# The passage from FFN1 into the mixer in one written order, and the first chunk's product in the gate's buffer

## The chip, the cores and the metric

One core of a Trainium2 chip runs the whole program in one launch. The metric is the time of the program on the device in microseconds (us); lower is better.

## The reference

One layer of a decoder on 512 tokens of width 1024, all in float32:

```
x = x + 1/2 * rms_norm(swiglu(rms_norm(x, ffn1_pre)), ffn1_post)
x = x +       rms_norm(mixer (rms_norm(x, mix_pre)),  mix_post)
x = x + 1/2 * rms_norm(swiglu(rms_norm(x, ffn2_pre)), ffn2_post)

rms_norm(x, g) = x * rsqrt(mean(x*x) + 1e-6) * g
swiglu(h)      = (silu(gate) * up) @ w_down      # gate, up = halves of h @ w_gu; 2 * 2816 columns
mixer(h):  z = h @ w_in                          # 512 pooling, 512 query, 2 * 128 key and value columns
           windowed pooling | 128-wide windowed attention, each rms-normed, then @ w_out
```

## The kernel before

Every matmul operand is split into a high part (a copy by ACT, L166) and a low part (raw minus high, by DVE or POOL, L169); a product is three matmuls, high by high, low by high and high by low (`mm3`, L359 to L361). The 512 tokens lie in 4 blocks `x0` to `x3` of 128.

An FFN has two stages. `gate_up` computes gate and up in 11 chunks of 256 columns. Chunk 0 is done plainly in eight blocks (names `f_c`; f1 and f2 stand for the two FFNs, and the profile writes f for both). Chunks 1 to 10 use a Strassen-like scheme of 7 products in the order 1, 5, 2, 6, 3, 7, 4, in pairs of banks px, py and pz (names f_x, f_y, f_z). They need sums of quarters of the normed input: `token_sums` forms them (`f1f`) and splits them into high and low parts `f1t5`, `f1t6`, `f1t7`, `f1t4` (low parts on DVE, L477). Behind chunk 0 ACT writes silu(gate) into two buffers `s00` and `s01` (tag `sg2`, which has two buffers), and DVE multiplies them by up (L541) into `hs`. The pairs of banks come free only when DVE has read chunk 0's banks, and ACT's first copy of a px (L587) goes into a buffer of tag `sg2` that the product has read.

`down_proj` computes 7 products of half the width in the order 1, 5, 6, 3, 7, 2, 4, from weight tiles `d`. The last product, 4, goes into the banks `xs_`; of its six weight tiles two are used for both halves of the tokens, then four (`tail`) for block 2 and again for block 3. Each block is then post-normed by `post_norm`: squares of both halves on ACT (`j_f1po`), the mean on DVE (`ms_f1po`, L339), the root on POOL (`r_f1po`, L334), gains (L413) and the sum into x (L416) on DVE. For f1 the mixer's pre-norm of the block follows (`j_b`, `r_b`, `xn_b`), and after that the normed block is transposed by PE (`tr_mx`) and split by ACT and DVE into `xT_hi` and `xT_lo` (L397, L400). The mixer's block 0 of queries (`pq0`, 24 matmuls of 512 columns) and of keys and values (`pkv0`, 24 of 256 columns) follows, with weights `wq0` to `wq3`, `wkv0`, `wkv1`; then block 1 (`pq1`, `pkv1`).

PE runs in the order in which the code is written. `in_order()` does the same for DVE, ACT and POOL; outside of it a scheduler orders those three when the program is built. Before the change the last product of `down_proj` and the passage into the mixer stand outside. Weights are loaded by SP's DMA queue in a fixed order (`W`), into eight buffers; `W.more(n)` issues loads and casts for n more, and `W.run_ahead` says how many loads go ahead of the casts. POOL's own DMA queue sums weights in `gate_up`. `power` is the root on POOL, and `pcols` is a transpose of 12 rows of factors into columns that the mixer's later parts read.

Of the kernel before, what the change touches and what calls it, by code (L numbers as in the profile page):

```python
# [10 lines left out]
F32 = mybir.dt.float32  # L11
# [8 lines left out]
P = 128  # L20
# [47 lines left out]
def trunk_layer(  # L68
# [262 lines left out]
    def power(ms, name):  # L331

        r = sm.tile([P, 1], F32, tag="r", name=f"r_{name}")
        nc.gpsimd.tensor_tensor(r, ms, half, ALU.pow)  # L334
        return r

    def mean_square(ss2, eps, name):
        ms = sm.tile([P, 1], F32, tag="ms", name=f"ms_{name}")
        nc.vector.scalar_tensor_tensor(ms, ss2[:, 0:1], eps, ss2[:, 1:2], ALU.add, ALU.add)  # L339
        return ms  # L340
# [39 lines left out]
                between()  # L380
        return xn

    def pre_norm(t, g, name, xn=None):
        r = power(mean_square(sizes(t, name), EPS, f"{name}{t}"), f"{name}{t}")
        return scaled(t, r, g, name, xn=xn)

    def transposes(t, xn, xT, name):
        for h in range(2):
            ps = bank(f"tr_{name}{t}{h}")
# [14 lines left out]
    def halves(g):  # L404
        return g[:, :512], g[:, 512:]

    def post_norm(t, parts, tmp, g, scale, name, dst=None):

        ss2 = squares(parts, ROOT / scale, f"{name}{t}")
        r = power(mean_square(ss2, EPS / (scale * scale), f"{name}{t}"), f"{name}{t}")  # L410
        for n in range(2):
            at = slice(n * 512, (n + 1) * 512)
            nc.vector.tensor_tensor(tmp[n], parts[n], g[:, at], ALU.mult)  # L413
        for n in range(2):
            at = slice(n * 512, (n + 1) * 512)
            nc.vector.scalar_tensor_tensor(xs[t][:, at], tmp[n], r, xs[t][:, at], ALU.mult, ALU.add)  # L416
            if dst is not None:
                nc.sync.dma_start(dst[:, at], xs[t][:, at])
# [39 lines left out]
    def token_sums(xq, name):  # L458

        parts, full = xq  # L460
        out = {1: parts[0, 0], 2: parts[1, 0], 3: parts[1, 1]}
        for p in (5, 6, 7, 4):
            out[p] = act_pair(f"{name}t{p}", (P, 4, 256))
        sums = {}
        for q in range(2):
            b11, b12, b21, b22 = (full[i][q] for i in ((0, 0), (0, 1), (1, 0), (1, 1)))
            nc.vector.tensor_tensor(b11, b11, b12, ALU.subtract)
            nc.vector.tensor_tensor(b12, b22, b12, ALU.subtract)
            nc.vector.scalar_tensor_tensor(b22, b22, -1.0, b11, ALU.mult, ALU.subtract)
            nc.vector.scalar_tensor_tensor(b21, b21, -1.0, b22, ALU.mult, ALU.subtract)  # L470
            sums[q] = {5: b11, 7: b12, 6: b22, 4: b21}
        for p in (5, 6, 7, 4):
            hi, lo = out[p]
            for q in range(2):
                at = (slice(None), slice(2 * q, 2 * q + 2))
                nc.scalar.copy(hi[at], sums[q][p])
                nc.vector.tensor_tensor(lo[at], sums[q][p], hi[at].bitcast(F32), ALU.subtract)  # L477
        return out

    def product_late(ps, w, xt, first, last):  # L480

# [23 lines left out]
    def gate_up(name, xq, hs, between):  # L505
# [18 lines left out]
                block(i)  # L524
        for i in range(4, 8):
            block(i)
        xs_ = token_sums(xq, name)
        W.hi, W.lo = nc.scalar, nc.vector
        W.run_ahead = 3
        W.more(2)  # L530
# [7 lines left out]
        for j in range(2):  # L538
            sg = wk.tile([P, 2, 256], F32, tag="sg2", bufs=2, name=f"{name}_s0{j}")
            nc.scalar.activation(sg, banks[0, j].rearrange("p (h t) -> p h t", h=2), AF.Silu, scale=-1.0)  # L540
            nc.vector.scalar_tensor_tensor(  # L541
                hs[0][:, 2 * j : 2 * j + 2, 0], banks[1, j].rearrange("p (h t) -> p h t", h=2), -1.0,
                sg, ALU.mult, ALU.mult,
            )
        use_banks(f"{name}_pairs", 4)

        def h_of(c):
# [65 lines left out]
        use_banks(f"{name}_banks", 8)  # L613
        return begin, [on_act[-1], on_dve[-1]]

    def down_proj(name, hs, ends, g_post, between, done):

# [49 lines left out]
                elif i == 2:  # L669
                    nc.vector.tensor_tensor(kept[1][:, t], zs_[t], kept[1][:, t], ALU.add)  # L670

        def normed(t):
            first = kept[1][:, t] if t < 2 else xs_[t - 2]
            second = kept[6][t] if t < 2 else kept[5][:, t - 2]
            dst = out[0, t * P : (t + 1) * P, :] if name == "f2" else None
            tmp = slots_of["pool"].tile([P, 512], F32, tag="k", bufs=2, name=f"{name}_n{t}") if t >= 2 else first
            post_norm(t, [first, second], [tmp, second], g_post, 0.5, f"{name}po", dst)
            done(t)

        NW = (NCH + 1) // 2  # L680
        with behind(ends[0]):
# [2 lines left out]
        with behind(ends[1]):  # L684
            form(1, 2)
            W.get(f"{name}_d10")
        with in_order():
            for at, i in enumerate(PRODUCTS[:-1]):
                for n in range(NW):
                    w = W.get(f"{name}_d{i}{n}")  # L690
                    if n % 2 == 0:
                        form(PRODUCTS[at + 1], n // 2)
                    multiply(i, n, w)
                    if n == 0 and at:
                        put_away(PRODUCTS[at - 1])
        i = PRODUCTS[-1]
        for n in range(2):
            multiply(i, n, W.get(f"{name}_d{i}{n}"))
            if n == 0:
                put_away(PRODUCTS[-2])  # L700
        normed(0)
        normed(1)
        tail = [W.get(f"{name}_d{i}{n}", 0) for n in range(2, NW)]
        if name == "f1":
            W.run_ahead = 3
            W.more(2)
        for t in range(2):
            for n, w in enumerate(tail):
                multiply(i, n + 2, w, (t,))
                if t and n == 1:  # L710
                    between(1)
            if t and name == "f1":
                W.more(2)
            normed(t + 2)
            if t == 0:
                between(0)
        use_slots(f"{name}_end", HB)


    xq = quarters("f1")  # L720
# [118 lines left out]
    xT2 = []  # L839
    xns = {}  # L840

    def done1(t):
        xn = ap.tile([P, 2, 512], F32, tag=("ahi", "alo")[t % 2], name=f"xn_b{t}")
        xns[t] = pre_norm(t, g3, "b", [xn[:, n] for n in range(2)])

    def between1(t):
        if t == 0:
            xT2.extend(act_pair(f"xT2_{i}") for i in range(4))
        transposes(t, xns[t], xT2, "mx")

    pcols = bank("pcols")
    nc.tensor.transpose(pcols[:, :12], rows, ident[:12, :12])
    nc.vector.tensor_copy(cols, pcols[:, :12])
    nc.vector.tensor_tensor(cols[:, 4:8], cols[:, 0:4], cols[:, 4:8], ALU.mult)
    down_proj("f1", hs, ends, g2, between1, done1)

    def project(ps, t, nm, per):
        for k in range(KD):
# [222 lines left out]
        next(pi[g])  # L1081

    def mixer():
        nc.scalar.copy(wph, wpr)
        nc.gpsimd.tensor_tensor(wpl, wpr, wph.bitcast(F32), ALU.subtract)
        qkv_block(0, lambda: None)
        qkv_out(0)
        transposes(2, xns[2], xT2, "mx")
        qkv_block(1, lambda: transposes(3, xns[3], xT2, "mx"))
        qkv_out(1)  # L1090
        turn(0)
        W.run_ahead = 2
        W.lo = nc.gpsimd
        qkv_block(2, lambda: (scores(0), tops(0), turn(1), exps(0, 0), exps(0, 1)))
        qkv_out(2)
        normalise(0)
        qkv_block(3, lambda: (W.more(2), scores(1), tops(1), turn(2), exps(1, 0)))
        W.more(2)
        turn_probs(0, 0)
        turn_probs(0, 1)  # L1100
        exps(1, 1)
        qkv_out(3)
        run(3)
        normalise(1)
        scores(2)
        run(3)
        tops(2)
        pool_sums(3)
        values(0, 0)
        values(0, 1)  # L1110
        turn(3)
        exps(2, 0)

        turn_probs(1, 0)
        attn_out(0)
        run(2)
        scores(3)
        exps(2, 1)
        tops(3, (0,))
        values(1, 0)  # L1120
        turn_probs(1, 1)
        normalise(2)
        tops(3, (1,))
        run(2)
        values(1, 1)
        pool_sums(2)
        W.lo = nc.vector

        turn_probs(2, 0)
        attn_out(1)  # L1130
        exps(3, 0)
        pool_mid(3)
        run(1)
        W.more(1)
        attn_rms(0)
        values(2, 0)
        turn_probs(2, 1)
        exps(3, 1)
        normalise(3)
        run(1)  # L1140
        pool_sums(1)
        yT[0:2] = [act_pair(f"yT{i}") for i in (0, 1)]
        pool_out(3, True)
        values(2, 1)

        turn_probs(3, 0)
        attn_rms(1)
        attn_out(2)
        W.more(1)
        pool_mid(2)  # L1150
        run(0)
        values(3, 0)
        turn_probs(3, 1)
        run(0)
        pool_sums(0)
        W.more(2)
        pool_out(2)
        values(3, 1)
        pool_mid(1)
        pool_mid(0)  # L1160
        attn_rms(2)
        attn_out(3)
# [118 lines left out]
    hs2 = []  # L1281
    ends = gate_up("f2", xq2, hs2, last_steps)
    g6 = gain(ffn2_post, "g6")
    down_proj("f2", hs2, ends, g6, lambda t: None, lambda t: None)


# [27 lines left out]
```

## Time and profile before

| | us |
|---|---|
| median of 3 runs (lowest, highest) | 867.23 (865.86, 867.49) |
| the profiled execution | 867.36 |
| its span in the trace | 865.6 |
| PE busy in it | 826.5 (95%) |
| DVE, ACT, POOL busy | 662.3, 468.3, 204.4 |
| mean granted clock of TensorE | 0.988 |

The engines are PE (matmuls), DVE (vector), ACT (scalar), POOL (GpSimd) and SP (which issues DMAs). A row of the timeline has the start, the duration, the engine, the line, the operation, its output and inputs, and in brackets how long the engine had been idle and what released it. A row of a group has the number of operations, the busy time, the mean in ns, and the idle time before them. A row of PE's waits has the total, the number and the longest. A row of a window has the stretch, the summed busy time and that of PE, PE's weight loads, DVE, ACT and POOL, then the granted clock, the DMA share and GB/s.

### The profile page before, as it was taken

The page shows a single profiled execution, that of the slowest core. Times are in us where ns is not written, and L with a number is a line of the kernel's source. Part 1 is how long each engine was busy: PE and PEld are TensorE (multiplying, and loading weights), DVE is VectorE, ACT ScalarE, POOL GpSimd, SP SyncE. Part 2 cuts the span into 40 slices and gives each one's busy share as a digit, 9 for nine tenths or more (in the row PEclk, how much of TensorE's full clock was granted, in tenths as well). Part 3 has the DMA queues.
Part 4 walks back from the last instruction along what each step waited for, and adds up shares of the span by engine and source line. Part 5 has one row for each costly group of instructions (what it writes and reads, how often), then busy time and mean ns, then how long its engine had stood idle before and what let it go on. Part 6 is the DMA issues. An engine that isn't in the chain of part 4 may idle for free. (4 is left out here: it accounts for less than half of the span.)

```text
span 865.6 us, 14043 instructions
## 1 busy us (share of the span) xinstructions
PE 826.5 (95%) x5525; PEld 755.2 (87%) x5525; DVE 662.3 (77%) x856; ACT 468.3 (54%) x743; POOL 204.4 (24%) x287
## 2 busy tenths in 40 slices
PE   7989999999999999789999998799999999999996
PEld 5889999999988878578878878799999999988785
DVE  6968887778987798744666779578888888877895
ACT  5644444454555575545996567344544445555662
POOL 4103334433310000123532011033333333300001
PEclk9999999999999999999999999999999999999999
DMA  9428888888885558312005402258899887955552
GB/s 305 122 69 217 230 233 221 225 235 237 233 262 182 183 190 260 110 28 71 26 25 147 145 25 74 66 159 237 222 240 232 235 241 221 252 198 173 175 163 97
DMA packets 96877, 150.77 MB, mean 174 GB/s; under 512 B 6948, under 2 KB 53676, under 8 KB 96812
## 3 DMA queue, kind: packets, MB, share of 16 engines
q1 hardware_dynamic: 77100, 103.74, 38.0%
q0 software_dynamic: 19712, 46.15, 22.5%
q8 instruction: 43, 0.70, 0.3%
q14 instruction: 22, 0.18, 0.1%
HBM read 147.77 MB, written 48.23 MB: 226 GB/s over the span
## 5 line engine op out<-in xcount | busy, mean ns | idle before, releaser
L571 POOL DMA_DIRECT2D f_t<-in_ffn_w_down x132 | 89.6, 751 | 80.7 <-issue 47.8
L169 DVE TENSOR_TENSOR f_d_lo<-f_d_raw,f_d_hi 128x1024 fp32r<-128x1024 f32 x84 | 92.1, 1130 | 8.8 <-ACT f_d_hi L166 8.1
L166 ACT CAST f_d_hi<-f_d_raw 128x1024 fp32r<-128x1024 f32 x84 | 79.0, 978 | 15.6 <-PE f_z L361 14.7
L568 POOL COPY f_k<-f_h 1x1 f32<-1x1 f32 x18 | 21.0, 1165 | 192.8 <-DVE f_h L560 192.8
L595 ACT COPY f_h<-f_y 128x512 f32<-128x512 f32 x20 | 11.7, 587 | 80.8 <-PE f_y L361 80.8
L603 ACT ACTIVATE f_s<-f_s 128x1024 f32<-128x1024 f32 x20 | 21.2, 1061 | 41.5 <-DVE f_s L602 41.5
L571 POOL DMA_DIRECT2D f_t<-f_t x44 | 32.1, 798 | 37.0 <-issue 30.6
L600 ACT COPY f_s<-f_x 128x512 f32<-128x512 f32 x20 | 11.7, 587 | 48.4 <-PE f_x L361 48.4
L635 ACT CAST f2e_hi<-f_h 128x1024 fp32r<-128x1024 f32 (+1 forms) x21 | 20.4, 977 | 30.9 <-DVE f_h L632 7.7
L635 ACT CAST f1e_hi<-f_h 128x1024 fp32r<-128x1024 f32 (+1 forms) x21 | 20.4, 976 | 30.9 <-DVE f_h L632 7.7
L359 PE MATMUL f_x<-f_d_hi,f1e_hi 128*128 128x512 f32 x88 | 35.1, 398 | 1.2 <-DVE f_h L611 1.2
L360 PE MATMUL f_x<-f_d_lo,f2e_hi 128*128 128x512 f32 x88 | 34.4, 391 | 0.8 <-DVE f_d_lo L169 0.8
L360 PE MATMUL f_x<-f_d_lo,f1e_hi 128*128 128x512 f32 x88 | 34.6, 393 | 0.5 <-DVE f_d_lo L169 0.5
L359 PE MATMUL f_x<-f_d_hi,f2e_hi 128*128 128x512 f32 x88 | 34.4, 390 | 0.7 <-DVE f_h L611 0.7
L587 ACT COPY f_s<-f_x 128x512 f32<-128x512 f32 x20 | 11.7, 586 | 42.5 <-PE f_x L361 39.8
L361 PE MATMUL f_x<-f_d_hi,f1e_lo 128*128 128x512 f32 x88 | 34.5, 392 | 0.0
L361 PE MATMUL f_x<-f_d_hi,f2e_lo 128*128 128x512 f32 x88 | 34.3, 389 | 0.0
L636 DVE TENSOR_TENSOR f1e_lo<-f_h,f1e_hi 128x1024 fp32r<-128x1024 f32 (+1 forms) x21 | 23.7, 1132 | 11.4 <-ACT f1e_hi L635 11.4
L636 DVE TENSOR_TENSOR f2e_lo<-f_h,f2e_hi 128x1024 fp32r<-128x1024 f32 (+1 forms) x21 | 23.6, 1133 | 11.4 <-ACT f2e_hi L635 11.4
L334 POOL TENSOR_TENSOR r_f1po<-ms_f1po,half 128x1 f32<-128x1 f32 x4 | 3.5, 865 | 107.8 <-DVE ms_f1po L339 107.8
L334 POOL TENSOR_TENSOR r_f2po<-ms_f2po,half 128x1 f32<-128x1 f32 x4 | 3.5, 865 | 106.6 <-DVE ms_f2po L339 106.6
L359 PE MATMUL po<-wo_hi,yT_hi 128*128 128x512 f32 x64 | 25.3, 395 | 0.0
(1026 smaller groups left out, 3421.8 us busy)
## 6 DMA issues: line engine op xcount, KB each, us to landing
f_t<-in_ffn_w_down POOLq DMA_DIRECT2D x132, 256.0 KB, 6.2
f_d_raw<-f_t SPq DMA_DIRECT2D x40, 512.0 KB, 4.6
f_d_raw<-in_ffn_w_down SPq DMA_DIRECT2D x30, 512.0 KB, 4.2
f_t<-f_t POOLq DMA_DIRECT2D x44, 256.0 KB, 6.6
f_raw<-in_ffn_w_gu SPq DMA_DIRECT2D x8, 512.0 KB, 7.6
x<-in_x SPq DMA_DIRECT2D x4, 512.0 KB, 8.2
f_d_raw<-f_t SPq DMA_DIRECT2D x8, 256.0 KB, 3.7
wq_raw<-in_w_in SPq DMA_DIRECT2D x4, 512.0 KB, 4.2
```

The lines of the kernel that those rows point to most:

```text
L166: nc.scalar.copy(hi, src)
L169: self.lo.tensor_tensor(lo, src, hi.bitcast(F32), ALU.subtract)
L359: nc.tensor.matmul(ps, wh, xh, start=first, stop=False, skip_group_check=open_)
L360: nc.tensor.matmul(ps, wh, xlo, start=False, stop=False, skip_group_check=open_)
L361: nc.tensor.matmul(ps, wlo, xh, start=False, stop=last, skip_group_check=open_)
L568: then = nc.gpsimd.tensor_copy(tick, hs[(c - 1) // 4][:1, 0, (c - 1) % 4, :1]).ins
L571: nc.gpsimd.dma_start(to, part, accum_op=op, max_dma_last_dim=2048)
L587: on_act.append(nc.scalar.copy(sg[:, :, a], px[:, :, a]).ins)
L595: on_act.append(nc.scalar.copy(h[1], py[:, :, a]).ins)
L603: on_act.append(nc.scalar.activation(sg, sg, AF.Silu, scale=-1.0).ins)
L635: nc.scalar.copy(hi, src)
L636: nc.vector.tensor_tensor(lo, src, hi.bitcast(F32), ALU.subtract)
```

## The change

- `gate_up`: the product up * silu(gate) of chunk 0 is written in place into the gate's buffer (L534 of the new program), and POOL copies it from there into `hs[0]` (L537). `token_sums` becomes a generator; it is left after the sums and product 5's split, and the splits for products 6, 7 and 4 come behind the second product.
- `down_proj`: `post_norm` and `pre_norm` are taken apart into sizes, gains, roots and sums. The squares of all blocks' second halves, and the gains of blocks 0 and 1's, are done during product 2; blocks 0 and 1 have their roots side by side. The squares of a whole FFN's post-norm share one tile.
- The passage: everything from the last product to `pq0`, `pkv0` and the norm of block 3 is in one `in_order()`, written by hand with `steps` that f1 hands in. The transposes of block 0 move from ahead of block 3's matmuls to behind the second of its four tiles, block 1's from there to behind its last tile, and block 2's from ahead of `pq1` to between `pq0` and `pkv0`. The weight casts come one at a time; `wq3_lo` and `wkv0_lo` are made by POOL instead of DVE. Block 3's sum, sizes and norm are in the mixer.
- The factor columns (`pcols`, a copy and a product on DVE) move from ahead of f1's `down_proj` into the mixer, ahead of `pq1`. On SP's queue the load of the pooling weights (`wpr`) moves from behind the `wu` loads to between `wkv0`'s and `wkv1`'s.
- FFN2 uses the same `down_proj` with no `steps`.

What the queues then hold, first DVE behind FFN2's first chunk. Before (`f2f101` is a sum of `token_sums`, `f2t` are splits, `f2_1b_raw` a sum of chunk 1's weights, `f2_h0` is `hs[0]`):

```order
L470 SCALAR_TENSOR_TENSOR f2f101_5365<-f2f101_5365,f2f111_5367 128x512
L477 TENSOR_TENSOR f2t6_lo_5754<-f2f110_5366,f2t6_hi_5753 128x512
L477 TENSOR_TENSOR f2t7_lo_5756<-f2f010_5362,f2t7_hi_5755 128x512
L219 TENSOR_TENSOR f2_1b_raw_5787<-f2_1a_raw_5501,f2_1b_raw_5787 128x1024
L477 TENSOR_TENSOR f2t7_lo_5756<-f2f011_5363,f2t7_hi_5755 128x512
L477 TENSOR_TENSOR f2t6_lo_5754<-f2f111_5367,f2t6_hi_5753 128x512
L477 TENSOR_TENSOR f2t4_lo_5758<-f2f100_5364,f2t4_hi_5757 128x512
L477 TENSOR_TENSOR f2t4_lo_5758<-f2f101_5365,f2t4_hi_5757 128x512
L541 SCALAR_TENSOR_TENSOR f2_h0_5808<-f2_c10_5586,f2_s00_5811 128x2x256
L541 SCALAR_TENSOR_TENSOR f2_h0_5808<-f2_c11_5611,f2_s01_5814 128x2x256
```

And after:

```order
L461 SCALAR_TENSOR_TENSOR f2f101_5367<-f2f101_5367,f2f111_5369 128x512
L534 SCALAR_TENSOR_TENSOR f2_s00_5801<-f2_c10_5588,f2_s00_5801 128x512
L219 TENSOR_TENSOR f2_1b_raw_5777<-f2_1a_raw_5503,f2_1b_raw_5777 128x1024
L534 SCALAR_TENSOR_TENSOR f2_s01_5805<-f2_c11_5613,f2_s01_5805 128x512
L470 TENSOR_TENSOR f2t6_lo_5756<-f2f110_5368,f2t6_hi_5755 128x512
L470 TENSOR_TENSOR f2t6_lo_5756<-f2f111_5369,f2t6_hi_5755 128x512
L470 TENSOR_TENSOR f2t7_lo_5758<-f2f010_5364,f2t7_hi_5757 128x512
```

The two products now stand ahead of all six low parts; the weight sum stands between them.

ACT in the passage, before (`wq` and `wkv` are the casts of weights, `j_b2` the squares of block 2's pre-norm, two for a block, `j_f1po` those of the post-norm, `xT2` the transposed blocks):

```order
L166 CAST wq2_hi_3894<-wq2_raw_3766 128x1024
L353 ACTIVATE j_b11_3752,ss2_b1_3749<-x1_89 128x512
L166 CAST wq3_hi_3900<-wq3_raw_3768 128x1024
L353 ACTIVATE j_f1po20_3803,ss2_f1po2_3802<-f1_x0_2945 128x512
L353 ACTIVATE j_f1po21_3805,ss2_f1po2_3802<-f1_p5_3221 128x512
L353 ACTIVATE j_b20_3817,ss2_b2_3816<-x2_90 128x512
L353 ACTIVATE j_b21_3819,ss2_b2_3816<-x2_90 128x512
L353 ACTIVATE j_f1po30_3906,ss2_f1po3_3905<-f1_x1_2946 128x512
L397 CAST xT2_0_hi_3827<-tr_mx00_3835 128x2x128
```

And after:

```order
L166 CAST wq2_hi_3851<-wq2_raw_3756 128x1024
L353 ACTIVATE j_b20_3858,ss2_b2_3857<-x2_90 128x512
L353 ACTIVATE j_b21_3860,ss2_b2_3857<-x2_90 128x512
L677 ACTIVATE j_f1po30_3871,f1_sso_2945<-f1_x1_2944 128x512
L393 CAST xT2_0_hi_3823<-tr_mx10_3879 128x2x128
L393 CAST xT2_1_hi_3825<-tr_mx10_3879 128x2x128
L393 CAST xT2_2_hi_3827<-tr_mx11_3888 128x2x128
L393 CAST xT2_3_hi_3829<-tr_mx11_3888 128x2x128
L166 CAST wq3_hi_3899<-wq3_raw_3758 128x1024
L166 CAST wkv0_hi_3945<-wkv0_raw_3771 128x1024
L166 CAST wkv1_hi_3960<-wkv1_raw_3849 128x1024
```

The cast `wq3_hi` stood ahead of the squares of block 2 and stands now behind them, block 3's first squares and the four high parts of block 1's transposes; `wkv0_hi` and `wkv1_hi` follow it directly.

POOL in the passage, before:

```order
L334 TENSOR_TENSOR r_f1po0_3717<-ms_f1po0_3715,half_106 128x1
L334 TENSOR_TENSOR r_b0_3731<-ms_b0_3729,half_106 128x1
L334 TENSOR_TENSOR r_f1po1_3742<-ms_f1po1_3740,half_106 128x1
L334 TENSOR_TENSOR r_b1_3756<-ms_b1_3754,half_106 128x1
L334 TENSOR_TENSOR r_f1po2_3809<-ms_f1po2_3807,half_106 128x1
L334 TENSOR_TENSOR r_b2_3823<-ms_b2_3821,half_106 128x1
L334 TENSOR_TENSOR r_f1po3_3912<-ms_f1po3_3910,half_106 128x1
L1085 TENSOR_TENSOR wpl_3941<-wpr_3938,wph_3940 128x512
L334 TENSOR_TENSOR r_b3_3926<-ms_b3_3924,half_106 128x1
```

And after:

```order
L334 TENSOR_TENSOR r_f1po0_3707<-ms_f1po0_3705,half_106 128x1
L334 TENSOR_TENSOR r_f1po1_3712<-ms_f1po1_3710,half_106 128x1
L334 TENSOR_TENSOR r_b0_3754<-ms_b0_3752,half_106 128x1
L334 TENSOR_TENSOR r_b1_3769<-ms_b1_3767,half_106 128x1
L334 TENSOR_TENSOR r_f1po2_3809<-ms_f1po2_3807,half_106 128x1
L334 TENSOR_TENSOR r_f1po3_3877<-ms_f1po3_3875,half_106 128x1
L169 TENSOR_TENSOR wq3_lo_3900<-wq3_raw_3758,wq3_hi_3899 128x1024
L169 TENSOR_TENSOR wkv0_lo_3946<-wkv0_raw_3771,wkv0_hi_3945 128x1024
L334 TENSOR_TENSOR r_b2_3951<-ms_b2_3949,half_106 128x1
L334 TENSOR_TENSOR r_b3_4040<-ms_b3_4038,half_106 128x1
L1155 TENSOR_TENSOR wpl_3915<-wpr_3912,wph_3914 128x512
```

Roots of blocks 0 and 1 now stand in pairs, and the two subtractions of 128x1024 stand ahead of block 2's root, for whose norm `xn_b2` the transposes between `pq0` and `pkv0` wait.

The diff, cut to its core:

```diff
         for p in (5, 6, 7, 4):
+            if p == 6:
+                yield out
...
-        xs_ = token_sums(xq, name)
+        to_sum = token_sums(xq, name)
+        xs_ = next(to_sum)
...
-            nc.vector.scalar_tensor_tensor(
-                hs[0][:, 2 * j : 2 * j + 2, 0], banks[1, j].rearrange("p (h t) -> p h t", h=2), -1.0,
-                sg, ALU.mult, ALU.mult,
+            done = nc.vector.scalar_tensor_tensor(
+                sg, banks[1, j].rearrange("p (h t) -> p h t", h=2), -1.0, sg, ALU.mult, ALU.mult
             )
+            nc.gpsimd.tensor_copy(hs[0][:, 2 * j : 2 * j + 2, 0], sg)
+        with behind([done.ins]):
+            next(to_sum, None)
...
+        sizes_ = sm.tile([P, 2 * NT], F32, tag="ls", bufs=2, name=f"{name}_sso")
+        tmp, rs = {}, {}
+        def half_of(t, n):
+            if t < 2:
+                return (kept[1][:, t], kept[6][t])[n]
+            return (xs_[t - 2], kept[5][:, t - 2])[n]
+        def half_size(t, n):
+            junk = wk.tile([P, 512], BF16, tag="junk", bufs=1, name=f"j_{name}po{t}{n}")
+            nc.scalar.activation(
+                junk, half_of(t, n), AF.Square, scale=2 * ROOT, accum_out=sizes_[:, 2 * t + n : 2 * t + n + 1]
+            )
+        def half_gain(t, n):
+            part = half_of(t, n)
+            tmp[t, n] = part
+            if t >= 2 and n == 0:
+                tmp[t, n] = slots_of["pool"].tile([P, 512], F32, tag="k", bufs=2, name=f"{name}_n{t}")
+            nc.vector.tensor_tensor(tmp[t, n], part, g_post[:, n * 512 : (n + 1) * 512], ALU.mult)
+        def post_root(t):
+            rs[t] = power(mean_square(sizes_[:, 2 * t : 2 * t + 2], 4 * EPS, f"{name}po{t}"), f"{name}po{t}")
+        def add_to_x(t):
             dst = out[0, t * P : (t + 1) * P, :] if name == "f2" else None
+            add_normed(t, (tmp[t, 0], tmp[t, 1]), rs[t], dst)
...
+        mix = steps if name == "f1" else {}
+        def then(step, t):
+            if step in mix:
+                mix[step](t)
...
+                    if i == 2 and 1 <= n <= 4:
+                        half_size(n - 1, 1)
+                        if n <= 2:
+                            half_gain(n - 1, 1)
+            i = PRODUCTS[-1]
+            w = W.get(f"{name}_d{i}0")
+            multiply(i, 0, w)
+            put_away(2)
+            for t in range(2):
+                half_size(t, 0)
+            for t in range(2):
+                half_gain(t, 0)
+                post_root(t)
+            w = W.get(f"{name}_d{i}1")
+            multiply(i, 1, w)
+            for t in range(2):
+                add_to_x(t)
+                then("size", t)
+            tail = [W.get(f"{name}_d{i}{n}", min(3, NW - 1 - n)) for n in range(2, NW)]
+            then("root", 0)
+            then("weights", 0)
+            then("norm", 0)
+            then("root", 1)
+            then("weights", 1)
+            then("norm", 1)
+            for t in (2, 3):
+                half_gain(t, 1)
             for n, w in enumerate(tail):
+                multiply(i, n + 2, w, (0,))
+            half_size(2, 0)
+            half_gain(2, 0)
+            post_root(2)
+            for n, w in enumerate(tail):
+                multiply(i, n + 2, w, (1,))
+                if n == 1:
+                    then("turn", 0)
+                    then("weights", 2)
+                    add_to_x(2)
+                    then("size", 2)
+            half_size(3, 0)
+            half_gain(3, 0)
+            post_root(3)
+            then("turn", 1)
+            then("weights", 3)
+            if not mix:
+                add_to_x(3)
...
+    def weights1(n):
+        W.run_ahead = 3
+        W.lo = nc.gpsimd if n == 3 else nc.vector
+        W.more(1)
...
     def mixer():
+        with in_order():
+            W.more(1)
+            W.lo = nc.vector
+            root1(2)
+            norm1(2)
+            add_to_x(3)
+            W.more(1)
+            size1(3)
+            qkv_block(0, lambda: turn1(2))
+            root1(3)
+            norm1(3)
         nc.scalar.copy(wph, wpr)
         nc.gpsimd.tensor_tensor(wpl, wpr, wph.bitcast(F32), ALU.subtract)
-        qkv_block(0, lambda: None)
         qkv_out(0)
-        transposes(2, xns[2], xT2, "mx")
+        pcols = bank("pcols")
+        nc.tensor.transpose(pcols[:, :12], rows, ident[:12, :12])
+        nc.vector.tensor_copy(cols, pcols[:, :12])
+        nc.vector.tensor_tensor(cols[:, 4:8], cols[:, 0:4], cols[:, 4:8], ALU.mult)
         qkv_block(1, lambda: transposes(3, xns[3], xT2, "mx"))
```

More of the change, by code (lines that the diff above doesn't have):

```diff
@@ L381, in scaled @@
         return xn
-    def pre_norm(t, g, name, xn=None):
-        r = power(mean_square(sizes(t, name), EPS, f"{name}{t}"), f"{name}{t}")
-        return scaled(t, r, g, name, xn=xn)
     def transposes(t, xn, xT, name):
@@ L405, in halves, with add_normed @@
         return g[:, :512], g[:, 512:]
[L407 to L413, printed above, removed]
+    def add_normed(t, tmp, r, dst=None):
         for n in range(2):
@@ L477, in token_sums @@
                 nc.vector.tensor_tensor(lo[at], sums[q][p], hi[at].bitcast(F32), ALU.subtract)
-        return out
     def product_late(ps, w, xt, first, last):
@@ L614, in gate_up, with down_proj @@
         return begin, [on_act[-1], on_dve[-1]]
-    def down_proj(name, hs, ends, g_post, between, done):
+    def down_proj(name, hs, ends, g_post, steps):
         forms = {}
@@ L670, in put_away @@
                     nc.vector.tensor_tensor(kept[1][:, t], zs_[t], kept[1][:, t], ALU.add)
-        def normed(t):
-            first = kept[1][:, t] if t < 2 else xs_[t - 2]
-            second = kept[6][t] if t < 2 else kept[5][:, t - 2]
+        sizes_ = sm.tile([P, 2 * NT], F32, tag="ls", bufs=2, name=f"{name}_sso")
[18 more added lines that the diff above has]
+        def add_to_x(t):
             dst = out[0, t * P : (t + 1) * P, :] if name == "f2" else None
-            tmp = slots_of["pool"].tile([P, 512], F32, tag="k", bufs=2, name=f"{name}_n{t}") if t >= 2 else first
-            post_norm(t, [first, second], [tmp, second], g_post, 0.5, f"{name}po", dst)
-            done(t)
+            add_normed(t, (tmp[t, 0], tmp[t, 1]), rs[t], dst)
         NW = (NCH + 1) // 2
@@ L695, in down_proj @@
                         put_away(PRODUCTS[at - 1])
[L696 to L707, printed above, removed]
-            for n, w in enumerate(tail):
[L709 to L716, printed above, removed]
+                    if i == 2 and 1 <= n <= 4:
+                        half_size(n - 1, 1)
+                        if n <= 2:
+                            half_gain(n - 1, 1)
@@ L717, in down_proj @@
+            half_size(3, 0)
[5 more added lines that the diff above has]
+                add_to_x(3)
         use_slots(f"{name}_end", HB)
+        return add_to_x
     xq = quarters("f1")
@@ L840, in trunk_layer, with size1, root1, norm1 @@
     xns = {}
-    def done1(t):
+    sizes1, roots1 = {}, {}
+    def size1(t):
+        sizes1[t] = sizes(t, "b")
+    def root1(t):
+        roots1[t] = power(mean_square(sizes1[t], EPS, f"b{t}"), f"b{t}")
+    def norm1(t):
         xn = ap.tile([P, 2, 512], F32, tag=("ahi", "alo")[t % 2], name=f"xn_b{t}")
-        xns[t] = pre_norm(t, g3, "b", [xn[:, n] for n in range(2)])
-    def between1(t):
+        xns[t] = scaled(t, roots1[t], g3, "b", xn=[xn[:, n] for n in range(2)])
+    def turn1(t):
         if t == 0:
@@ L849, in between1 @@
         transposes(t, xns[t], xT2, "mx")
[L851 to L855, printed above, removed]
+    def weights1(n):
+        W.run_ahead = 3
+        W.lo = nc.gpsimd if n == 3 else nc.vector
+        W.more(1)
+    add_to_x = down_proj(
+        "f1", hs, ends, g2,
+        {"size": size1, "root": root1, "norm": norm1, "turn": turn1, "weights": weights1},
+    )
     def project(ps, t, nm, per):
@@ L1283, in trunk_layer @@
     g6 = gain(ffn2_post, "g6")
-    down_proj("f2", hs2, ends, g6, lambda t: None, lambda t: None)
+    down_proj("f2", hs2, ends, g6, {})
 _INS = [
```

## The prediction, on record before the changed kernel ran

> **What bounds the kernel now.** I read the page's busy shares first, then PE's waits by length, then windows round each long wait, and last the timeline of the engine that PE waits for.
>
> ```profile
> span 865.6 us, 14043 instructions
> PE 826.5 (95%) x5525; PEld 755.2 (87%) x5525; DVE 662.3 (77%) x856; ACT 468.3 (54%) x743; POOL 204.4 (24%) x287
> PE f_x L359 <- DVE f_h L541: 4.6, 1, 4.6
> PE tr_mx L391 <- DVE xn_b L378: 3.9, 1, 3.9
> PE f_y L359 <- ACT f_s L587: 3.2, 1, 3.2
> ```
>
> PE is busy for 826.5 of 865.6 us, so a change that leaves the matmuls alone can win only PE's idle time and what idling does to its clock. Three waits stand out, and the change is at all three: one behind each FFN's first chunk (f_y, f_x) and one in the passage from FFN1 into the mixer (tr_mx). Windows show what follows each; the columns wanted are PE's busy time, the fifth engine's after it, and PEclk.
>
> ```profile
> 46.64:50.98 4.34, 4.34 (x25) 4.34 (x25) 1.23 (x1) 0.89 (x1) 0.00 (x0) 0.64 0.22 56
> 50.98:53.86 2.88, 2.88 (x27) 2.88 (x25) 1.06 (x1) 2.48 (x3) 0.00 (x0) 1.00 0.28 97
> 547.83:552.27 4.44, 4.44 (x24) 4.44 (x25) 0.00 (x0) 0.00 (x0) 0.00 (x0) 0.62 0.02 4
> 356.92:360.62 3.70, 3.70 (x14) 3.27 (x14) 3.26 (x6) 0.54 (x2) 0.86 (x1) 0.54 0.59 177
> 374.00:377.40 3.40, 3.40 (x19) 3.40 (x18) 1.41 (x2) 0.23 (x1) 0.55 (x1) 0.51 0.00 0
> 339.04:377.99 38.95, 30.35 (x140) 24.89 (x138) 29.18 (x50) 21.36 (x52) 7.29 (x10) 0.91 0.38 115
> ```
>
> The 24 matmuls behind the first stall took 4.34 us at a granted clock of 0.64; the next 24 took 2.88 at 1.00, so the stall cost 1.46 more than itself. Behind the second it is 4.44, 1.56 more. The last row is the passage, from the start of the last product to the first matmul of pq1 (the mixer's second query product): 38.95 us, of which PE idles 8.60. The two rows above it lie inside: 3.70 us at 0.54 and 3.40 at 0.51, together some 3.4 us lost to the clock.
>
> **Part A, FFN1's first chunk.** DVE's timeline, and PE's first row after the stall:
>
> ```profile
> 39.67 0.68 DVE L477 TENSOR_TENSOR f1t_lo<-f1f,f1t_hi 128x512 fp32r<-128x512 f32 x1
> 40.27 1.21 DVE L219 TENSOR_TENSOR f_1b_raw<-f_1a_raw,f_1b_raw 128x1024 f32<-128x1024 f32 x1
> 41.41 0.68 DVE L477 TENSOR_TENSOR f1t_lo<-f1f,f1t_hi 128x512 fp32r<-128x512 f32 x1
> 42.01 0.68 DVE L470 SCALAR_TENSOR_TENSOR f1f<-f1f,f1f 128x512 f32<-128x512 f32 x1
> 42.61 2.48 DVE L477 TENSOR_TENSOR f1t_lo<-f1f,f1t_hi 128x512 fp32r<-128x512 f32 x4
> 45.20 1.29 DVE L541 SCALAR_TENSOR_TENSOR f_h<-f_c,f_s 128x512 f32<-128x512 f32 x2
> 46.64 0.55 PE L359 MATMUL f_y<-f1t_hi,f_1p_hi 128*128 128x256 f32 x1 [3.17 <-ACT f_s L587]
> ```
>
> PE stops at 43.47 and starts at 46.64, 0.15 us after the second product (L541) ends: f_y needs the bank that the product frees, so I read the wait as DVE's, though the row names ACT's copy L587, which itself waits for that product. Six low parts (L477), 0.6 us apart, stood ahead of the products and now stand behind. From 39.67 DVE then does the weight sum (1.14 to the next start) to 40.81, the first product to 41.42, L470 to 42.02, the second product to 42.71. PE needs it at 43.47, so there is no stall and nothing cools: 3.17 + 1.46 = 4.63, taken as 4.6. With the clock's part kept it is 3.2.
>
> The new POOL copies into h are not in this trace. The nearest rows are POOL's:
>
> ```profile
> L169 POOL TENSOR_TENSOR f_c_lo<-f_raw,f_c_hi 128x512 fp32r<-128x512 f32 x7 | 10.4, 1506 | 1.0 <-ACT f_c_hi L166 0.8
> L169 POOL TENSOR_TENSOR wu_lo<-wu_raw,wu_hi 128x1024 fp32r<-128x1024 f32 x4 | 9.5, 2390 | 3.7 <-ACT wu_hi L166 3.7
> L1043 POOL TENSOR_TENSOR win<-u 128x511 f32<-128x511 f32 x4 | 4.2, 1038 | 20.5 <-ACT u L1037 20.5
> ...
> L334 POOL TENSOR_TENSOR r_b<-ms_b,half 128x1 f32<-128x1 f32 x4 | 2.2, 548 | 11.9 <-DVE ms_b L339 11.9
> ```
>
> A copy has one input fewer than L1043's 1.04 us, and at most costs f_c_lo's 1.51; I take 1.0. Only ACT's next px copy waits for it: s00's copy starts at 41.4 and ends by 42.9, before the product for px has ended, so it costs nothing. The six low parts run from 42.71 to 46.3; the first two (product 6) end near 44.0, and that product comes 48 matmuls of 0.12 after 43.47, at 49.2. Five microseconds of cover hide them.
>
> **Part B, FFN2's first chunk.**
>
> ```profile
> 541.05 0.69 DVE L470 SCALAR_TENSOR_TENSOR f2f<-f2f,f2f 128x512 f32<-128x512 f32 x1
> ...
> 542.86 1.22 DVE L219 TENSOR_TENSOR f_1b_raw<-f_1a_raw,f_1b_raw 128x1024 f32<-128x1024 f32 x1
> ...
> 546.40 1.28 DVE L541 SCALAR_TENSOR_TENSOR f_h<-f_c,f_s 128x512 f32<-128x512 f32 x2
> 547.83 0.36 PE L359 MATMUL f_x<-f2b_hi,f_1p_hi 128*128 128x256 f32 x1 [4.60 <-DVE f_h L541]
> ```
>
> Here DVE does L470 until 541.66, the first product, then the weight sum from 542.27 to 543.41 (the order keeps it between the products), the second product to 544.10, and PE starts 0.15 later at 544.25 instead of 547.83: 3.58 won. PE idles about 1.0 us instead of 4.60, which I expect to cool nothing: 1.56 more, 5.14 in all, taken as 5.1; 3.6 with the clock's part kept.
>
> **Part C, the passage.** Taken away: nothing but a few shared tiles. Moved: squares and gains of second halves into an earlier product, both first roots side by side, the block transposes later, weight casts one at a time, wq3's and wkv0's low parts from DVE to POOL, and x3's norm into the mixer. What POOL does to DVE is seen here:
>
> ```profile
> 415.67 2.38 POOL L169 TENSOR_TENSOR wu_lo<-wu_raw,wu_hi 128x1024 fp32r<-128x1024 f32 x1
> 417.15 0.92 DVE L966 TENSOR_TENSOR ls<-ls,es 128x8 f32<-128x8 f32 x1 [1.17 <-ACT st L960]
> ```
>
> A DVE operation of 8 columns with two SBUF inputs lasted 0.92 and ended (418.07) with POOL's (418.05): it was held off until POOL was done. I take POOL behind DVE to fare alike. The Trainium skill has this on "SBUF — State Buffer", in the section on its two separate sides: the pair of ports that both engines use is an exclusive lock, and the loser blocks. The two rows agree with it.
>
> PE's longest wait between pq0 and pq1, and durations for the schedule:
>
> ```profile
> PE pkv L359 <- ACT wkv_hi L166: 1.2, 1, 1.2
> L400 DVE TENSOR_TENSOR xT_lo<-tr_mx,xT_hi 128x256 fp32r<-128x256 f32 x16 | 5.6, 417 | 7.3 <-ACT xT_hi L397 7.3
> L169 DVE TENSOR_TENSOR wq_lo<-wq_raw,wq_hi 128x1024 fp32r<-128x1024 f32 x4 | 4.9, 1223 | 2.1 <-ACT wq_hi L166 2.1
> L416 DVE SCALAR_TENSOR_TENSOR x<-f_p,r_f1po,x 128x512 f32<-128x512 f32 x6 | 4.3, 748 | 0.9 <-POOL r_f1po L334 0.9
> L353 ACT ACTIVATE j_b<-x 128x512 bf16<-128x512 f32 x8 | 5.0, 630 | 12.6 <-DVE x L416 12.5
> L397 ACT CAST xT_hi<-tr_mx 128x256 fp32r<-128x256 f32 x16 | 4.7, 401 | 5.1 <-PE tr_mx L391 5.1
> L166 ACT CAST wq_hi<-wq_raw 128x1024 fp32r<-128x1024 f32 x4 | 4.2, 1038 | 0.7 <-PE f_x L361 0.7
> ```
>
> From 339.04 PE runs 66 matmuls, 0.227 apart, and two groups of transposes (0.79 warm), to 355.58 if nothing stops it. DVE, with those durations: x0 and x1 summed by 346.2, xn_b0 by 351.5 (its transposes are due at 351.96), xn_b1 by 354.65 (due 354.79). The 3.9 wait for xn_b thus goes, with 0.14 to spare. What is late next: xT_lo of block 0, behind block 2's and 3's gains, 356.5 to 357.9 (PE waits 0.85 inside pq0); wq2_lo to 359.0; x2's sum to 360.4. ACT then squares x2 (361.2), squares block 3 (361.95), writes xT_hi of block 1 (363.1) and only then casts wq3 (364.1); pq0 reached wq3 at 360.5, so PE waits 3.6. POOL's two low parts of 2.39 end at 366.5 (PE waits 2.2 more) and 368.9; block 2's root stands behind them (369.4), and half of xn_b2 is there at 370.2, for which the moved transposes wait 1.7. Idle comes to 0.85 + 3.6 + 2.2 + 1.7 = 8.35, as much as the 8.60 before; waits are exchanged. After 370.2 come eight transposes (0.8 warm, 1.6 at half clock), the 24 matmuls of pkv0 (2.9 as in the row of 50.98, 4.4 as in that of 547.83) and pcols (0.1): pq1 starts between 374.0 and 376.3, against 377.99. PE has by then idled in three pieces, so I take the clocked-down end and a little for the handovers: 376.5, a gain of 1.5. Bounds: +4.0 if all is warm; if each POOL subtraction needs 3.0 instead of 2.39 (twice f_c_lo's 1.506), xn_b2 slips by 1.2 to 371.4, and at the slow clock pq1 starts at 377.7, a gain of 0.3; twice 3.5 takes it below nothing, to −0.7.
>
> The moved pcols transposes and its two column operations on DVE have their readers far behind; before, they stood ahead of f1's down product where PE had other work: nothing either way. SP's order puts the wpr load between wkv0's and wkv1's; wkv1 then lands near 351, wanted near 364: hidden.
>
> **Part D, the end of FFN2.**
>
> ```profile
> 858.98 0.69 DVE L413 TENSOR_TENSOR f_n<-f_x,g 128x512 f32<-128x512 f32 x1 [1.38 <-ACT j_f2po L353]
> 860.04 0.86 POOL L334 TENSOR_TENSOR r_f2po<-ms_f2po,half 128x1 f32<-128x1 f32 x1 [3.89 <-DVE ms_f2po L339]
> ```
>
> The second half's square and gain leave the tail, but f_n still waits for ACT's read of the same bank, so the mean starts no earlier than before by more than 0.1. The root has no gain beside it (DVE's second one ran under it before): r_b's 0.55 for 0.86, 0.3 won. Bounds −0.1 and 0.7 (a whole gain, too).
>
> **The sum.** 4.6 + 5.1 + 1.5 + 0.3 = 11.5. The profiled execution took 867.36 (span 865.6 and 1.76 round it), 0.13 above the median of 867.23: 867.36 − 11.5 = 855.9.
>
> **Rivals.** (1) POOL is slower in the passage than its rows, 3.5 us a subtraction: C = −0.7, the sum 9.3, 858.1. For it: DVE is busy beside POOL there nearly all the time; against it: wu_lo's mean of 2.39. (2) The passage stays warm: C = 4.0, the sum 14.0, 853.4. Against it: 374.00:377.40 ran at 0.51 though no wait in the 4 us before was over 1.2. The Trainium skill, "TensorE: Matmul & The Clock Gate", Part 1, says that the clock halves only after at least one idle window of about 3.4 us; by that rule the pieces of idle above, shorter or barely as long, cool almost nothing, which gives this rival's 853.4. The trace disagrees, with 0.51 behind 1.2 and 0.64 behind 3.17. (3) One first chunk's stall stays, because f_y really waits for ACT's copy as the row says, or POOL's copy into h blocks the next sums: A = 0, the sum 6.9, 860.5. Against it: L587 can't start before L541. (4) The reordering does nothing, because the scheduler's order already bound nothing: 867.4; the stalls above speak against it. (5) Slower: POOL becomes the bound of the passage. The two low parts would have to eat the whole 11.5, 5.75 each, so 8.1 us instead of 2.39; from there on the time is over 867. The longest POOL operation of this kind here is far below.
>
> **Chances.** Forecast 0.59, rival 1 0.18, rival 2 0.13, rival 3 0.05, no change 0.03, slower 0.02. About 0.2% (1.7 us) is what a measurement of this kernel tells from no change, so faster means below 865.5: 0.95, same 0.03, slower 0.02. The range takes in rivals 1 and 2 with some of A's and B's clock part kept on the high side (858.1 + 1.9) and D's bound on the low side (853.4 − 0.4 and as much for the runs): 852.6 to 860.0.
>
> **What would show it.** In the changed profile no wait of f_y in FFN1's pairs, one of about 1 us in FFN2's, both windows of 24 matmuls at 2.9; pq0 waiting for wq3's high part and then for POOL's wq3_lo, tr_mx for xn_b2, about 2 to 4 us each; wq3_lo and wkv0_lo near 2.4 us; the end from last matmul to last sum 0.3 shorter. I am wrong if the stalls behind the first chunk reappear on ACT's px copy, if xn_b1 misses its 0.14 of slack by much, or if the clock of the passage is other than taken.

## The result and the profile after

The changed kernel takes 854.22 us (median of 4 runs, 853.71 to 854.52) against 866.55 for the kernel before on the same chips: a ratio of 0.9857 (95% interval 0.984 to 0.9874), 12.3 us less; 11.5 were forecast. The forecast of 855.9 is 1.7 high, 0.8 of it because it was counted from 867.36 and the kernel before came out at 866.55 in these runs.

The page of the changed kernel, and PE's waits in it (total, number, longest):

```profile
span 851.9 us, 14057 instructions
PE 822.5 (97%) x5525; PEld 751.8 (88%) x5525; DVE 661.0 (78%) x854; ACT 467.5 (55%) x743; POOL 213.2 (25%) x293
...
PE pq L359 <- ACT wq_hi L166: 3.2, 1, 3.2
PE pq L360 <- POOL wq_lo L169: 1.9, 1, 1.9
...
PE f_x L359 <- DVE f_s L534: 1.6, 1, 1.6
...
PE tr_mx L387 <- DVE xn_b L378: 1.1, 1, 1.1
```

The wait of 3.2 for FFN1's f_y is gone, FFN2's shrank from 4.6 to 1.6, and the passage's 3.9 for xn_b has given way to three waits at pq0 and the transposes behind it. The same windows as before: the 24 matmuls behind each first chunk, then the half-clock stretch and the whole of the passage (columns as ahead).

```profile
43.11:45.99 2.88, 2.88 (x27) 2.88 (x25) 2.88 (x5) 0.00 (x0) 0.00 (x0) 1.00 0.20 71
536.14:539.08 2.94, 2.94 (x25) 2.94 (x26) 2.94 (x6) 0.00 (x0) 1.12 (x1) 1.00 0.63 184
359.43:369.67 10.24, 8.05 (x31) 7.04 (x32) 5.36 (x10) 4.03 (x11) 4.36 (x4) 0.50 0.22 67
333.88:370.67 36.79, 30.54 (x140) 25.23 (x138) 26.31 (x49) 20.18 (x47) 12.15 (x11) 0.86 0.42 132
```

Both groups of 24 run at full clock. The passage went from 38.95 to 36.79 us; PE idles 6.25 in it instead of 8.60, but 10.24 us of it instead of 6.83 are at half clock.

Between the two profiled executions (spans 865.6 and 851.9, 13.7 apart; that of before was 0.8 above its median, that of after 0.5 below) the time divides so: FFN1's first chunk 4.79 (from the first f_x matmul to the end of the 24 behind the stall, 10.55 to 5.76), FFN2's 4.46 (from the end of chunk 0 likewise, 9.04 to 4.58), the passage 2.16, the end of FFN2 0.46 (from the last matmul's start to the end of the span, 7.81 to 7.35), and 1.8 elsewhere. Of that, 1.4 lies between pq1 and the end of FFN2's chunk 0, where PE's work was not changed: in the trace of before a half-clock window stands there (531.07 to 534.48), in that of after none.

### The profile page after: what moved, and what is told of

It reads as the page before. It is cut to its first block, busy times and chain, and to the rows that moved or that the text cites. A ratio compares the mean times of both kernels' runs of the same rounds, so it can differ in the third digit from the quotient of the medians.

```text
span 851.9 us, 14057 instructions
## 1 busy us (share of the span) xinstructions
PE 822.5 (97%) x5525; PEld 751.8 (88%) x5525; DVE 661.0 (78%) x854; ACT 467.5 (55%) x743; POOL 213.2 (25%) x293
```

## The experiments

**Each half alone.** The first kernel is the one before with the gate_up part alone (the diff's first three pieces), the second the changed kernel with those three pieces undone.

> The kernel before with the first part of the change alone: product in the gate's buffer, POOL's copy, split of products 6, 7 and 4 behind the second product; passage, down product and factor columns as before. Theory: the two stalls behind the first chunks carry most of the gain; FFN1's goes (4.6 to 4.8 us with its clock part), FFN2's shrinks from 4.60 to about 1.6 and no longer cools (4.5): 9 us below before, about 857.3. Rival: most of the gain came from the passage and the clock there; then this is within 3 us of before, 863.5 or more.

> The changed kernel with the old first chunk (product written to h, all low parts of the token sums ahead of it); the passage in its written order and the factor columns as changed. Theory: the passage gains 2.2 us as in the trace (38.95 to 36.79) and the end of FFN2 0.5, so 863.8, and the stalls of 3.2 and 4.6 us behind the first chunks are back. Rival 1 of the prediction (POOL eats the passage's gain): 865.5 to 866.5.

The first took 855.43 us (0.9879, 0.9858 to 0.9899), 10.9 below before, the second 864.11 (0.997, 0.996 to 0.998), 2.2 below. In PE's waits of the first, FFN1's stall is gone, FFN2's is 1.6, and the passage's is as it was:

```profile
PE tr_mx L391 <- DVE xn_b L378: 3.9, 1, 3.9
...
PE f_x L359 <- DVE f_s L543: 1.6, 1, 1.6
```

The first was expected at 857.3 and is 1.9 faster, the second at 863.8. Nearly all of the gain is gate_up's, and the medians add up (13.1 against 12.3 together, with runs of one kernel up to 3.5 us apart). The traces show more. In that of the first, the two first chunks give what they give in the changed kernel (4.79 and 4.45), but FFN2's chunk 0 is 1.50 us shorter than before (31.23 to 29.73, without its half-clock window), and so is the passage, in which no line was edited:

```profile
334.82:372.27 37.45, 31.02 (x139) 25.08 (x138) 29.20 (x50) 21.13 (x51) 7.10 (x10) 0.86 0.37 119
```

So the passage's edit shortens the passage by 0.66 us where gate_up is changed already (37.45 to 36.79) and by 2.33 where it isn't (38.95 to 36.62 in the second kernel's trace). Why the unedited passage came out shorter is not shown; its waits and its half-clock windows (10.24 us instead of 6.83) lie differently.

**The order or the buffer.**

```diff
         xs_ = next(to_sum)
+        next(to_sum, None)
...
-        with behind([done.ins]):
-            next(to_sum, None)
```

> The changed kernel with one thing undone: the splits of the token sums for products 6, 7 and 4 are written ahead of the two products again, while the products still go in place into the gate's buffer and POOL still copies. Theory: only DVE's order counts, so PE waits for the second product behind five or six low parts again, 3 us and more in each FFN with the clock's part behind it: 7 to 9 us above the changed kernel, 861 to 863. Rival: the new buffer is what frees the banks early, the order is of no weight: 854 as the changed kernel.

862.28 us (0.995, 0.9935 to 0.9965), 8.1 above the changed kernel and within the 861 to 863 expected. PE's first rows behind the two chunks:

```profile
45.98 0.50 PE L359 MATMUL f_y<-f1t_hi,f_1p_hi 128*128 128x256 f32 x1 [2.35 <-DVE f_s L535]
...
543.40 0.55 PE L359 MATMUL f_x<-f2b_hi,f_1p_hi 128*128 128x256 f32 x1 [4.65 <-DVE f_s L535]
```

With the gate's buffer and POOL's copies kept, but five of the six low parts ahead of the second product, the stalls are back: the order on DVE frees the banks. The buffer is what permits that order. POOL's copies in the changed kernel show it, though both products were done by 42.5:

```profile
42.39 3.69 DVE L470 TENSOR_TENSOR f1t_lo<-f1f,f1t_hi 128x512 fp32r<-128x512 f32 x6
46.21 1.17 POOL L537 COPY f_h<-f_s 128x512 f32<-128x512 f32 x2 [21.38 <-PE f_y L361]
46.85 0.59 ACT L582 COPY f_s<-f_x 128x512 f32<-128x512 f32 x1 [4.33 <-POOL f_h L537]
```

They start 0.13 us after the last low part ends at 46.08. `hs` lies where the token sums lay, and in the program the first copy waits for the last low part that reads them (PE, which the row names, had long been done). By the same reasoning a product straight into `hs` would wait as long, with PE behind it; no run tried that with the new order. ACT's px copy waits 4.33 us for POOL's and ends at 47.44; product 6 into the same banks starts at 48.87, so it costs nothing.

**POOL's chain in the passage.** The low parts of wq3 and wkv0 go back to DVE, in the same places:

```diff
-        W.lo = nc.gpsimd if n == 3 else nc.vector
+        W.lo = nc.vector
```

> The changed kernel with wq3_lo and wkv0_lo made by DVE at the same places of the order instead of POOL. Theory: POOL's chain wq3_lo, wkv0_lo, root of block 2 (2.35 + 2.36 + 0.55 us) is what ends last in the passage while DVE idles 5.14 us; on DVE each takes 1.13, the root of block 2 comes at once, block 2's transposes start 2.5 to 3 us earlier and the wait for wq3_lo shrinks from 1.93 to about 0.8: 850.5 to 852. Rival (the port between POOL and DVE): DVE's other work is what is late, and giving it 2.3 us more of work costs time: 855 to 856.

852.28 us (0.9832, 0.9817 to 0.9847), 1.9 below the changed kernel and just above the 850.5 to 852 expected. In the changed kernel, DVE and POOL while PE waits:

```profile
358.10 2.35 POOL L169 TENSOR_TENSOR wq_lo<-wq_raw,wq_hi 128x1024 fp32r<-128x1024 f32 x1 [0.62 <-ACT wq_hi L166]
360.41 2.36 POOL L169 TENSOR_TENSOR wkv_lo<-wkv_raw,wkv_hi 128x1024 fp32r<-128x1024 f32 x1
362.73 0.55 POOL L334 TENSOR_TENSOR r_b<-ms_b,half 128x1 f32<-128x1 f32 x1
363.31 1.41 DVE L378 SCALAR_TENSOR_TENSOR xn_b<-x,r_b,g 128x512 f32<-128x512 f32 x2 [5.14 <-POOL r_b L334]
```

DVE idles 5.14 us while POOL makes what DVE makes in half the time. With DVE doing it, PE's wait for wq3_lo is 0.47 and that for xn_b 0.18; the wait of 3.18 for ACT's cast of wq3 stays. The passage is 3.6 us shorter than the changed kernel's 36.79:

```profile
334.65:367.85 33.20, 29.37 (x141) 23.84 (x139) 27.70 (x50) 20.18 (x47) 6.02 (x8) 0.90 0.49 147
```

The time shows only 1.9 of it. In this trace two half-clock windows stand further on, at 440.01 in the mixer and 521.93 in FFN2's chunk 0, which the changed kernel's trace doesn't have; no line was edited there. So POOL's low parts cost 3.6 us in the passage and some 2 in the time.

**Casts earlier.** Two kernels were written; in the second, the root and norm of block 2 also stand first in the mixer:

```diff
                     then("weights", 2)
+                    then("weights", 3)
+                    then("weights", 3)   # second kernel only
                     add_to_x(2)
...
             then("turn", 1)
-            then("weights", 3)
```

> The changed kernel with wq3's cast (ACT) and low part (POOL) right behind wq2's, ahead of block 2's sum, where ACT idles 4.21 us; wkv0's stay where they are. Theory: both waits inside pq0 (3.20 and 1.93) go, but block 2's root still stands behind wkv0_lo on POOL, so its transposes start near 362.1 instead of 364.1 of the changed kernel's axis: 2 us less, about 852; PE's idle time is then one wait of some 6 us for xn_b. Rival: ACT's cast of wq3 was the whole price, and 5 us come off: 849.

> The changed kernel with wq3's and wkv0's casts and low parts right behind wq2's, still low parts on POOL, wkv1's cast there too, and block 2's root and norm ahead of what is left. Theory: the order of ACT and POOL behind block 2's squares, not the work, is what is late; xn_b2 is then ready near 358.9 instead of 364.1, one wait of about 3 us is left in the passage and at most two windows of half clock: 5 to 7 us below the changed kernel, 847 to 849.5. Rival: contention of POOL with DVE, which is busy there, gives the time back: 852 or more.

850.65 (0.9819, 0.9802 to 0.9837) and 850.75 us (0.9821, 0.9804 to 0.9839). The queues of ACT, POOL and DVE came out the same in both, with wkv0's and wkv1's casts early, so the first is no partial step and its expectation, 852, was about another order. The second was expected at 847 to 849.5. Its passage is 1.75 us shorter than the changed kernel's:

```profile
334.69:369.73 35.04, 28.89 (x140) 24.29 (x138) 29.70 (x49) 20.19 (x47) 12.86 (x11) 0.90 0.42 137
```

Why that is so little stands in its timelines of POOL and DVE:

```profile
352.05 2.40 POOL L169 TENSOR_TENSOR wq_lo<-wq_raw,wq_hi 128x1024 fp32r<-128x1024 f32 x1
354.41 3.36 POOL L169 TENSOR_TENSOR wkv_lo<-wkv_raw,wkv_hi 128x1024 fp32r<-128x1024 f32 x1
352.63 2.90 DVE L169 TENSOR_TENSOR wq_lo<-wq_raw,wq_hi 128x1024 fp32r<-128x1024 f32 x1
355.45 2.87 DVE L407 SCALAR_TENSOR_TENSOR x<-f_n,r_f1po,x 128x512 f32<-128x512 f32 x1
358.25 0.74 DVE L407 SCALAR_TENSOR_TENSOR x<-f_p,r_f1po,x 128x512 f32<-128x512 f32 x1
```

The two engines take turns: DVE's wq2_lo starts at 352.63, is held off until POOL ends at 354.45, and takes its 1.1 us; POOL's second subtraction starts at 354.41 and is held off until DVE ends at 355.53; x2's first half sum waits for that one's end at 357.77 and ends at 358.32. x2 is complete at 358.99, 3.8 us later than in the changed kernel (354.36, on an axis 0.8 us earlier), and PE waits 5.14 us for xn_b2. The rival was right about the cause. Its price, 852 or more, looks too high, but 1.86 us of the gain are not the passage's: in both traces FFN2's first f_x starts without the wait of 1.64, and from the end of its chunk 0 to the end of the 24 matmuls it is 2.72 us instead of 4.58. In the second it starts at 533.34, and DVE begins the second product only at 534.30, so there f_x does not need the bank that this product frees. No line was edited there, and why it is so isn't shown.

**The order, without POOL.** Casts early as above, low parts on DVE behind x2's sum, the mean of block 2 between them (comments added; the helpers and the lines that go from the mixer are left out):

```diff
                     add_to_x(2)
+                    then("weights", 3)   # low part on DVE
+                    then("casts", 2)     # wkv0, wkv1: high parts alone
                     then("size", 2)
+                    then("root", 2)
+                    then("low", 0)       # low part of wkv0
+                    then("norm", 2)
             half_size(3, 0)
             half_gain(3, 0)
             post_root(3)
+            then("low", 1)
             then("turn", 1)
-            then("weights", 3)
```

> The changed kernel with the casts of wq3, wkv0 and wkv1 behind wq2's on ACT as in the early-cast runs, but every low part of these weights on DVE, behind block 2's sum; block 2's mean stands between wq3_lo and wkv0_lo, its norm behind wkv0_lo, and POOL does roots alone. Theory (the pair of ports: with POOL out of the way wq2_lo takes 1.2 instead of 2.9 and the first half of x2's sum 0.75 instead of 2.87): on the changed kernel's axis x2 is summed at 354.3, block 2's transposes start near 357.4 instead of 364.1, PE's waits in the passage are together under 3 us, and little or nothing of it runs at half clock: 844 to 847. Rival: the sum of DVE's work, not the port, is late, and the passage is no shorter than with POOL's help: 850 or more.

848.71 us (0.9786, 0.9773 to 0.98), above the 844 to 847 expected, though the passage did what was expected of it:

```profile
353.53 1.21 DVE L172 TENSOR_TENSOR wq_lo<-wq_raw,wq_hi 128x1024 fp32r<-128x1024 f32 x1
354.66 0.74 DVE L417 SCALAR_TENSOR_TENSOR x<-f_n,r_f1po,x 128x512 f32<-128x512 f32 x1
...
335.57:363.93 28.36, 26.97 (x141) 22.10 (x139) 25.30 (x44) 16.60 (x36) 7.71 (x7) 1.00 0.55 170
```

wq2_lo takes 1.21 and x2's half 0.74, and the passage is 28.36 us, 8.4 less than in the changed kernel, all at full clock. Neither step alone does that: 33.20 with the low parts on DVE, 35.04 with the casts early, 28.36 with both. Part of it comes back right behind pq1, where block 3's transposes now wait and take 1.3 us longer in all (from pq1's start to pkv1's, 7.7 instead of 6.4):

```profile
370.32 0.63 PE L397 MATMUL tr_mx<-ident,xn_b 128*128 128x128 f32 x4 [0.64 <-DVE xn_b L388]
371.25 0.63 PE L397 MATMUL tr_mx<-ident,xn_b 128*128 128x128 f32 x4 [0.30 <-DVE cols L1174]
```

Against the gain stand also two half-clock windows, at 27.31 in FFN1's chunk 0 and at 436.91 in the mixer, neither of which is in the changed kernel's trace; no line was edited there.

**The weight sum behind the second product.** `W.product` is that product.

```diff
         def plus(to, x, y):
-            nc.vector.tensor_tensor(raw[key[to]], raw[key[x]], raw[key[y]], ALU.add)
+            with behind([W.product] if c == 1 and to == "b" else []):
+                nc.vector.tensor_tensor(raw[key[to]], raw[key[x]], raw[key[y]], ALU.add)
```

> The changed kernel with the weight sum f_1b_raw of chunk 1 held until behind the second product, in both FFNs. Theory: the wait of FFN2's first f_x falls from 1.64 to about 0.5, nothing else: 1.1 us less, 853.1. Rival: the sum is late for product 3 or holds off POOL's copy and with it ACT's copy of px; then the waits come back among the pairs and the time is 854 or more.

853.11 us (0.9851, 0.9835 to 0.9866). The wait of FFN2's first f_x falls from 1.64 to 0.88 and not to the 0.5 expected, because DVE's second product now itself has to wait for PE's last matmul of chunk 0:

```profile
535.15 0.69 DVE L535 SCALAR_TENSOR_TENSOR f_s<-f_c,f_s 128x512 f32<-128x512 f32 x1 [0.28 <-PE f_c L479]
535.99 0.35 PE L360 MATMUL f_x<-f2b_hi,f_1p_hi 128*128 128x256 f32 x1 [0.88 <-DVE f_s L535]
```

The median is 1.1 below the changed kernel's, as expected, though the trace gives a reason for 0.76 alone; the intervals overlap, so the size isn't shown.

> The same, with the weight sum f_1b_raw behind the second product as well. Theory: the two add up, 1.1 us below the former: 843 to 846. Rival: the shift only moves a window of half clock, and the two are equal within 0.5 us.

Both edits together take 845.96 us (0.9759, 0.9746 to 0.9772), 2.75 below the passage's edit alone, in the expected range. That is more than the 0.76 that the sum's edit gives; the rest lies, in the traces, in the stretches of the two half-clock windows at 27.31 and 436.91, which are gone. The wait of block 3's transposes behind pq1 is still there. It is the fastest kernel of the study, 20.7 us below the kernel before. Its passage is as short as that of the former, and between 20 us and the last product its trace has no half-clock window at all:

```profile
333.70:362.05 28.35, 26.94 (x140) 22.08 (x139) 25.28 (x44) 16.60 (x36) 7.71 (x7) 1.00 0.54 170
```

## Why the prediction was right, and where it was off

- Part A, 4.6 forecast, 4.79 measured; the order on DVE was foreseen to 0.3 us (second product to end at 42.71, it ended at 42.47). The start of POOL's copies was wrong: 41.4 to 42.9 was said, they ran at 46.21. The text missed that `hs` shares memory with the token sums. The cover held, but for ACT's px copy it was 1.4 us and not the five that were named for the low parts.
- Part B, 5.1 forecast, 4.46 measured. The remaining wait is 1.64 and not 1.0: chunk 0 ran without the half-clock window it had before, so from that chunk's start PE came to the stall 1.5 us earlier, and DVE's second product ended only 0.9 earlier than scheduled. What B lost, the 1.4 elsewhere gave; it isn't a term of the sum, so that the sum came out is in part luck.
- Part C, 1.5 forecast, 2.16 measured. The waits came where they were put: 3.20 for wq3's cast (3.6 said), 1.93 for POOL's low part (2.2), 1.12 for xn_b2 (1.7), while the 0.85 for xT_lo did not come. Idle time did not stay at 8.35 but fell to 6.25. The clocked-down end was the right choice: half clock held from 359.43 to 369.67. The step that was mis-sized is DVE's, which was ahead of the schedule by half a microsecond and more from the first sums on. That the size of C came out is luck too: with gate_up changed alone, the unedited passage already lost 1.50 of the 2.16, and for that the prediction has no term.
- Part D, 0.3 forecast, 0.46 measured; the last root took 0.55 instead of 0.86, and the mean came 0.15 sooner.
- Rival 2, the passage all warm, did not happen: half clock came at 359.43 behind waits of 3.20 and 1.93, of which 2.91 us lay in the window of 3.41 before. The rule that the Trainium skill gives in "TensorE: Matmul & The Clock Gate", Part 1, that the clock falls after an idle window of about 3.4 us, again did not fit: that window was not idle throughout. Rival 3 is refuted by the changed kernel itself and by the run with gate_up's part alone, which have no stall in FFN1, and rivals 4 and 5 by the time. POOL's subtractions took 2.35 and 2.36, so rival 1 was not the case either; but the passage was bound by them, as the run with the low parts on DVE shows.

## What to carry to other kernels

What frees a bank for PE belongs ahead of everything on its engine that has slack, and if the result's place isn't free yet, an intermediate buffer with a later copy buys that order. Work given to POOL was no relief here while DVE ran operations with two SBUF inputs (a subtraction of 1.21 us took 2.90 beside POOL's): look at what both do in the same stretch, and at who waits for POOL's next root. After removing a stall, search for the next one in the written order too: the same operations in another order, with two subtractions back on DVE, took the passage from 36.8 to 28.4 us, of which 1.3 came back behind it. And measure an edit in the stretches that it doesn't touch as well: here they moved by 1.5 us at a time.

## What the hardware showed beyond that

The granted clock changes on a grid of 3.41 us and only between full and half. I put the grid over the 11 traces (from 20 us to the last product) and counted PE's idle time in each window. At full clock, all 15 windows with 2.1 us or more of idle time were followed by half clock; of the 17 with 1.5 to 1.8, 5 were; of some 35 with 0.9 to 1.5, 2 (both had under 1.0, and none of the longer ones did); of some 90 with 0.4 to 0.9, none. So idle time per window decides most cases but not all. At half clock, 13 windows with 0.9 or more of idle time were all followed by another; of 23 with less, 22 were followed by full clock. Whether one given gap cools PE thus depends in part on how the grid cuts it, and this shifts with all that comes ahead: the trace of before has 5 half-clock windows, that of the changed kernel 3, the last kernel's none. A window of continuous matmuls at half clock costs half its length, 1.7 us. So an edit can show its gain in the passage and lose part of it 70 us later, as the second-last kernel did at 436.91; that the grid alone makes the scatter between runs was not tried, since each kernel has one trace.
